# Nine instead of seven pairs of an up projection by Strassen's products, some of them one behind another, and silu as one activation

## The chip, the cores and the metric

The kernel runs on one core of a Trainium2 chip. The metric is the device time of one execution in microseconds (us). Three timed runs of the kernel before took 867.1, 866.76 and 868.9 us; their median is 867.1. One more execution was profiled, and its trace is what the views below are made from.

## The reference

The reference is one block of a decoder: a recurrent branch and an attention branch that are merged, and then a feed-forward part with a short causal convolution. The change touches the feed-forward part alone:

```
h2 = rmsnorm(x, norm2_g[l]) * (1.0 + scale2) + shift2
u = causal_dwconv(h2 @ w_up[l], ffn_conv_w[l], ffn_conv_b[l])
u_gate, u_val = u[..., :D_FF], u[..., D_FF:]
x = x + gate2 * ((jax.nn.silu(u_gate) * u_val) @ w_down[l])
```

There are 512 tokens, a model width of 1024 and D_FF = 2816; the convolution has three taps along the tokens. All of it is float32.

## The kernel before, in words

**Products in three passes.** TensorE multiplies in fp32r. To keep float32's precision, `split` (L207) cuts an operand into two parts: ScalarE copies it into fp32r (L210), and VectorE subtracts this from the operand to get the rest (L211). A product then is three matmuls: high by high, high by low, low by high (`mm3`, L247 to L249).

**The up projection.** The 2 x 2816 output channels lie on partitions, in 44 tiles of 128 channels by 512 tokens. A pair `j` (0 to 21) is the gate's tile and the value's tile of the same 128 channels, `2j` and `2j+1`. A tile that is done the plain way takes eight blocks of the inner dimension by three passes, 24 matmuls of 512 columns, and its weights are two units of 128x512 that `Stream.get` (L226) loads and splits. `project` (L257) issues it. Its two tiles are in two banks of PSUM of the tag "acc", and `conv` (L1155) reads them there: one activation with scale and bias on ScalarE (L1157) and two scalar_tensor_tensor on VectorE (L1159). `gate` (L1161) makes silu(gate) x value and splits the result for the down projection: a tanh on ScalarE (L1162), two scalar_tensor_tensor on VectorE (L1163, L1164), and a split.

**A pair by Strassen's products.** The pairs in the list `STRASSEN` see the pair's two weight tiles and the two halves of the tokens as a 2 x 2 product of blocks, in Winograd's form: seven products of four blocks of the inner dimension by three passes, each 12 matmuls of 256 columns (`prod`, L1102). `weights` (L1111) loads the pair's two weight tiles into two buffers `raw` (L1115, L1116), makes four sums of quarters on VectorE (L1120, L1121, L1122, L1124) and splits seven quarters. The token side's sums (`Ts`) are made once, while pairs 0 to 3 run. `front` (L1128) issues six products into three banks, x of the tag "acc" and y and z of the tag "tr", and combines them in the pair's working tile `w`; `last_product` (L1149) adds the seventh, from the quarter `q22`, on top of what is in bank x. The combined outputs lie in `w` in SBUF, and `conv` and `gate` work from there.

**The order of the work.** Before the feed-forward part, the order of every engine's queue is written out by hand (`QUEUES`, `queue_order`). Within it a planner orders each engine's instructions by priorities; `high_priority(offset=AHEAD)` moves `weights` and the loads and splits of `project` 100 places ahead. TensorE's order is fixed by `in_order` (L253): each product is issued behind the last instruction noted in `chained`. The loop over pairs (L1170) issues `front` of a Strassen pair and goes on; the next pair is a plain one, and after that pair's first tile come the Strassen pair's `last_product`, its two `conv` and its `gate`. The next Strassen pair's `weights` are called at the plain pair's second tile. So Strassen pairs and plain pairs take turns from pair 5 to pair 17.

**Buffers that are waited for.** Split quarters and units lie in two buffers of the tag "whl" and two of "whg", by turns; `raw` has three buffers of 512 KB; the working tiles `w` (tag "Y") have two; "acc" and "tr" have three banks each.

**After it** comes the down projection, 12 of its 22 blocks of the inner dimension plainly and ten by Strassen's products (`f_forms`, `w_forms`, `strassen_down`), then the last norm and the output.

Of the kernel before, what the change touches and what calls it, by code (L numbers as in the profile page):

```python
# [14 lines left out]
AF = mybir.ActivationFunctionType  # L15
ALU = mybir.AluOpType
ADD, SUB, MUL = ALU.add, ALU.subtract, ALU.mult
# [73 lines left out]
AHE = 100  # L91
SQB = (1, 0, 2, 3)
EARLY = 4
STRASSEN = (5,7,9,11,13,15,17)
G2J = 18
ROOM = -1

# [74 lines left out]
def block_kernel(ctx, tc, a):  # L172
    nc = tc.nc
    V, S, G, PE = nc.vector, nc.scalar, nc.gpsimd, nc.tensor
# [25 lines left out]
    def raw():  # L200
        return st(sb, "raw", RAW, [P, 1024])
# [49 lines left out]
    chained = None  # L251

    def in_order(on=True):  # L253

        return tc.issue_after(chained) if on and chained is not None else ExitStack()
# [322 lines left out]
    with phase("p_attn") as p1:  # L578
# [5 lines left out]
        w = st(p1, "v", 2, [P, 2, T])  # L584
# [200 lines left out]
        for hd in range(HEADS):  # L785
            g, i = divmod(hd, 4)
# [65 lines left out]
    with phase("p_rnn") as p2:  # L852
# [87 lines left out]
        for m in range(8):  # L940
            b = bank("tr")
            project(b, wpr, m, NR, lambda k: yr[k], ahead=AHM, order=m >= ORDM)
            t = tr_[m]
# [22 lines left out]
        for k in range(NK):  # L966
            with tc.high_priority(offset=AHO):
                w, _ = wo.get(k * T)
# [3 lines left out]
            chained = last  # L972
# [12 lines left out]
        for t in range(4):  # L985
            b = bank("fil" if t % 2 else "gm")
            for k in range(NK):
                with tc.high_priority(offset=AHO):
                    w, _ = wo.get((NK + k) * T)
                with in_order(ORDO):  # L990
                    last = mm_tok(b, mg[k], tok(t), w, k == 0, k == NK - 1)
            chained = last
# [45 lines left out]
    with phase("p_ffn") as p3:  # L1038
# [4 lines left out]
        for s in (slice(0, T // 2), slice(T // 2, T)):  # L1043
            for m in range(EARLY):
                for k in range(NK):
                    with tc.high_priority(offset=AHE):
                        w, o = wu.get((m * NK + k) * P)
                    with in_order(ORDE):
                        last = mm3(ub[m][:, s], w, o, P, h2[:, k], s, k == 0, k == NK - 1)
                chained = last  # L1050
# [6 lines left out]
        HT, HK = T // 2, NK // 2  # L1057
# [18 lines left out]
        Ts = []  # L1076
# [25 lines left out]
        def prod(out, w, x, start, stop):  # L1102
            for k, (xk, s) in enumerate(x):

                wh, wl = w[:, 0, k * P:k * P + P], w[:, 1, k * P:k * P + P]
                for e, (we, xe) in enumerate(((wh, 0), (wh, 1), (wl, 0))):
                    last = PE.matmul(out, we, xk[:, xe, s], start=start and k == 0 and e == 0,  # L1107
                                     stop=stop and k == HK - 1 and e == 2, skip_group_check=True).ins
            return last

        def weights(j):  # L1111

            with tc.high_priority(offset=AHEAD):
                r0, r1 = raw(), raw()
                dma(r0, a["w_up"][2 * j])  # L1115
                dma(r1, a["w_up"][2 * j + 1])  # L1116
                w11, w12, w21, w22 = r0[:, :T], r0[:, T:], r1[:, :T], r1[:, T:]
                s1 = st(p3, "ff", NF, [P, T])
                q11, q12 = quarter(j, w11), quarter(j, w12)
                V.tensor_tensor(s1, w21, w22, ADD)  # L1120
                V.tensor_tensor(w21, w11, w21, SUB)  # L1121
                V.tensor_tensor(w11, s1, w11, SUB)  # L1122
                qs1, qs2 = quarter(j, s1), quarter(j, w11)
                V.tensor_tensor(w12, w12, w11, SUB)  # L1124
                qs4, qs3, q22 = quarter(j, w12), quarter(j, w21), quarter(j, w22)
            return q11, q12, qs1, qs2, qs4, qs3, q22

        def front(w, q11, q12, qs1, qs2, qs4, qs3, q22):  # L1128

            nonlocal chained  # L1130
            X, Y_, Z = bank("acc"), bank("tr"), bank("tr")
            x, y_, z = (b[:, :HT] for b in (X, Y_, Z))
            p1, p2, p5 = w[:, 2, :HT], w[:, 2, HT:], w[:, 3, :HT]
            with in_order():
                prod(x, q11, h_part(0, 0), True, False)
                prod(y_, q12, h_part(1, 0), True, True)
                S.activation(p1, x, AF.Copy)
                prod(z, qs1, Ts[0], True, False)
                V.tensor_tensor(w[:, 0, :HT], y_, p1, ADD)
                prod(x, qs2, Ts[1], False, False)  # L1140
                S.activation(p5, z, AF.Copy)
                prod(z, qs4, h_part(1, 1), False, True)
                S.activation(p2, x, AF.Copy)
                V.tensor_tensor(w[:, 0, HT:], z, p2, ADD)
                chained = prod(x, qs3, Ts[2], False, False)
                V.tensor_tensor(w[:, 1, HT:], x, p5, ADD)
            return x, q22

        def last_product(w, x, q22):  # L1149
            nonlocal chained  # L1150
            with in_order():
                chained = prod(x, q22, Ts[3], False, True)
            S.activation(w[:, 1, :HT], x, AF.Copy)

        def conv(j, i, u, src):  # L1155
            cj = i * NF + j
            S.activation(u, src, AF.Identity, scale=vc("fw", 2 * 2 * NF + cj), bias=vc("fb", cj))  # L1157
            for d in (1, 2):
                V.scalar_tensor_tensor(u[:, d:], src[:, :T - d], vc("fw", (2 - d) * 2 * NF + cj), u[:, d:], MUL, ADD)  # L1159

        def gate(u0, u1, t):  # L1161
            S.activation(t, u0, AF.Tanh, scale=0.5)  # L1162
            V.scalar_tensor_tensor(u0, t, 1.0, u0, ADD, MUL)  # L1163
            V.scalar_tensor_tensor(u0, u0, 0.5, u1, MUL, MUL)  # L1164
            o = hl(p3, "ff", NF)
            split(o, 0, T, u0)
            ff.append(o)

        left = None
        for j in range(NF):  # L1170
            w = st(sb, "Y", 2, [P, 4, T])
            if j in STRASSEN:
                left = (j, w) + front(w, *ahead)
                continue
            convs = []
            for i in range(2):
                if 2 * j + i < EARLY:
                    b = ub[2 * j + i]
                else:
                    b = bank("acc")  # L1180
                    project(b, wu, 2 * j + i, NK, lambda k: h2[:, k], ahead=AHEAD, order=ORD)
                if left and i == 0:
                    last_product(*left[1:])
                    for e in range(2):
                        conv(left[0], e, left[1][:, 2 + e, :], left[1][:, e, :])
                    gate(left[1][:, 2, :], left[1][:, 3, :], left[1][:, 0, :])
                    left = None
                if i and j + 1 in STRASSEN:
                    ahead = weights(j + 1)
                convs.append((j, i, w[:, i, :], b))  # L1190
            for c in convs:
                conv(*c)
            gate(w[:, 0, :], w[:, 1, :], w[:, 2, :])
            if j < 4:
                Ts.append(next(t_it))
            if j == G2J:
                g2_it = ada2(1, st(sb, "acc4", 1, [P, D]), lambda: st(sb, "R", 4, [P, D]))
            if G2J <= j < G2J + 4:
                next(g2_it)
                g2 = next(g2_it)  # L1200
            if j == G2J + 3:
                ada_row(g2, 1.0)
                fg = st(sb, "R", 4, [P, D])
                dma(fg, a["fg"].partition_broadcast(P))
                V.tensor_scalar(fg[:, T:], fg[:, T:], -0.5, None, MUL)
# [93 lines left out]
        for k in range(KO):  # L1299
            with tc.high_priority(offset=AHEAD):  # L1300
                w, _ = wd.get(k * T)
# [10 lines left out]
        for t in range(4):  # L1312
            w = xf[t]
# [16 lines left out]
        for k in range(KO - LASTK):  # L1330
            with tc.high_priority(offset=AHEAD):
                w, _ = wd.get((NF + k) * T)
# [8 lines left out]
        for part in parts:  # L1341
            t, o, n, b = part
            if o == 0:
                w = st(sb, "Y", 2, [P, 2, T])
# [115 lines left out]
```

## Time and profile before

| what | value |
|---|---|
| median of three timed runs | 867.1 us (866.76 to 868.9) |
| the profiled execution, its own time | 870.13 us |
| its span, first to last instruction | 868.3 us |
| mean granted TensorE clock | 0.994 |
| the 145.5 us from the first Strassen product to the last | 557.5 to 703.0 us of the span |

The profile page gives busy time by engine, the span in 40 slices, DMA queues, the chain of work that ended last, and groups of instructions by line. PE is TensorE's matmuls, PEld its weight loads, DVE VectorE, ACT ScalarE, POOL GpSimd, SP the queue that issues most DMAs. Times in the timeline count from the span's start. A matmul's length in the timeline holds its way through the array and overlaps the next, so a series is measured from the start of one to the start of the next. The same holds, in part, for VectorE: an instruction's length and its distance to the next are two numbers.

### The profile page before, as it was taken

Reading aid. Unit: us, or ns where it says so; the run is one execution under the profiler, and the core shown is the slowest. Engines: PE = TensorE matmul, PEld = TensorE weight load, DVE = VectorE, ACT = ScalarE, POOL = GpSimd, SP = SyncE. Lnnn points to the kernel's source line nnn. Section 1 sums busy time; section 2 is a strip of 40 time slices with the busy share of each in tenths; the row PEclk is TensorE's granted clock in tenths of the full one; section 3 lists DMA queues with packets and bytes.
Section 4 is the critical chain, followed back from the end, with each engine's and each line's share of the span. In section 5 each row is a group of like instructions: output and inputs, shape, how many; then the busy total and the mean of one; then the engine's idle time right before and its main releaser. Section 6 shows DMA issues by size and latency. Waiting matters only on the chain.

```text
span 868.3 us, 12376 instructions
## 1 busy us (share of the span) xinstructions
PE 845.7 (97%) x4432; PEld 698.3 (80%) x4432; DVE 737.1 (85%) x1417; ACT 534.8 (62%) x998; POOL 23.9 (3%) x49
## 2 busy tenths in 40 slices
PE   7999999999999999999999999999999999999995
PEld 4777888878877777777877798888888887889985
DVE  7989888988856899998375679999989999998985
ACT  7485878677745798886244566656666654535533
POOL 0001000001020000000000001000000000000000
PEclk8999999999999999999999999999999999999998
DMA  9913232443463243345324044322322374323332
GB/s 352 352 68 107 72 111 97 125 146 116 145 176 118 82 161 121 122 161 204 94 76 146 25 134 111 98 75 101 105 101 102 102 275 162 97 73 98 100 95 97
DMA packets 34674, 110.72 MB, mean 128 GB/s; under 512 B 4386, under 2 KB 8098, under 8 KB 34612
## 3 DMA queue, kind: packets, MB, share of 16 engines
q1 hardware_dynamic: 32116, 103.60, 35.1%
q0 software_dynamic: 2496, 6.33, 3.4%
q8 instruction: 35, 0.57, 0.3%
q14 instruction: 27, 0.22, 0.1%
HBM read 105.16 MB, written 2.13 MB: 124 GB/s over the span
## 4 chain that ended last, share of the span: by engine, by line
PE 55%; DVE 20%; ACT 10%; DMA 9%; issue 4%; POOL 0%; SPq 0%; ACTq 0%; DVEq 0%; POOLq 0%
PE acc L249 5%; PE acc L248 5%; PE acc L247 5%; PE tr L249 3%; PE tr L247 3%; PE tr L248 3%; DVE whg L211 3%; PE acc L1107 2%; DVE whl L211 2%; DMA wa<-in_w_adat 2%; PE tr L1107 2%; PE tr L749 2%; PE gm L249 2%; DVE Y L1159 1%; PE gm L247 1%
## 5 line engine op out<-in xcount | busy, mean ns | idle before, releaser
L210 ACT ACTIVATE whl<-raw 128x512 fp32r<-128x512 f32 (+2 forms) x149 | 83.6, 566 | 69.6 <-PE tr L249 22.4
L211 DVE TENSOR_TENSOR whl<-raw,whl 128x512 fp32r<-128x512 f32 (+2 forms) x149 | 90.6, 612 | 23.3 <-ACT whl L210 22.8
L210 ACT ACTIVATE whg<-raw 128x512 fp32r<-128x512 f32 x131 | 80.9, 625 | 44.5 <-PE tr L249 9.1
L211 DVE TENSOR_TENSOR whg<-raw,whg 128x512 fp32r<-128x512 f32 x131 | 89.2, 688 | 17.8 <-ACT whg L210 17.4
L726 ACT ACTIVATE P<-P,mx,qsc 128x512 f32<-128x512 f32 (+3 forms) x64 | 41.1, 645 | 17.4 <-DVE mx L722 17.3
L247 PE MATMUL acc<-A,whg 128*128 128x512 f32 x120 | 47.9, 399 | 0.0
L248 PE MATMUL acc<-A,whg 128*128 128x512 f32 x120 | 47.4, 395 | 0.0
L249 PE MATMUL acc<-A,whg 128*128 128x512 f32 x120 | 47.4, 395 | 0.0
L1159 DVE SCALAR_TENSOR_TENSOR Y<-acc,vec,Y 128x511 f32<-128x511 f32 (+1 forms) x58 | 43.0, 745 | 4.1 <-ACT Y L1157 4.1
L248 PE MATMUL acc<-A,whl 128*128 128x512 f32 x104 | 41.1, 395 | 0.0
L247 PE MATMUL acc<-A,whl 128*128 128x512 f32 x104 | 41.1, 395 | 0.0
L249 PE MATMUL acc<-A,whl 128*128 128x512 f32 x104 | 41.1, 395 | 0.0
L249 PE MATMUL gm<-A,whg 128*128 128x512 f32 x88 | 35.2, 400 | 1.9 <-DVE whg L211 1.9
L247 PE MATMUL gm<-A,whg 128*128 128x512 f32 x88 | 35.5, 404 | 0.0
L248 PE MATMUL gm<-A,whg 128*128 128x512 f32 x88 | 35.3, 401 | 0.0
L249 PE MATMUL tr<-A,whl 128*128 128x512 f32 x80 | 32.2, 403 | 1.2 <-DVE whl L211 1.1
L247 PE MATMUL tr<-A,whl 128*128 128x512 f32 x80 | 32.4, 406 | 0.6 <-ACT whl L210 0.6
L719 DVE CUSTOM_DVE_ANT_0 P<-acc,mask 128x384 f32<-128x384 f32 (+3 forms) x64 | 28.5, 486 | 4.0 <-PE acc L716 3.6
L248 PE MATMUL tr<-A,whl 128*128 128x512 f32 x80 | 31.5, 394 | 0.0
L210 ACT ACTIVATE ff<-Y 128x512 fp32r<-128x512 f32 (+1 forms) x27 | 15.9, 590 | 22.0 <-DVE Y L1164 20.8
L211 DVE TENSOR_TENSOR pt<-tr,pt 128x512 fp32r<-128x512 f32 (+1 forms) x48 | 27.5, 596 | 2.1 <-ACT pt L210 1.6
L749 PE MATMUL tr<-pt,v 128*128 128x512 f32 (+3 forms) x128 | 28.2, 328 | 0.1
(603 smaller groups left out, 2524.9 us busy)
## 6 DMA issues: line engine op xcount, KB each, us to landing
raw<-in_w_up SPq DMA_DIRECT2D x44, 512.0 KB, 3.6
raw<-in_w_dn SPq DMA_DIRECT2D x22, 512.0 KB, 3.5
wa<-in_w_adat SPq DMA_DIRECT2D x16, 512.0 KB, 9.4
raw<-in_w_adat SPq DMA_DIRECT2D x16, 512.0 KB, 3.3
raw<-in_w_xr SPq DMA_DIRECT2D x10, 512.0 KB, 3.8
raw<-in_w_pr SPq DMA_DIRECT2D x10, 512.0 KB, 3.6
raw<-in_w_gm SPq DMA_DIRECT2D x8, 512.0 KB, 4.0
raw<-in_w_gr SPq DMA_DIRECT2D x8, 512.0 KB, 3.5
```

Source lines behind the costliest of these rows:

```text
L210: S.activation(h, src, AF.Copy)
L211: return V.tensor_tensor(dst[:, 1, lo_c:lo_c + n], src, h.bitcast(F32), SUB).ins
L247: PE.matmul(out, wh, x[:, 0, xs], start=start, stop=False)
L248: PE.matmul(out, wh, x[:, 1, xs], start=False, stop=False)
L249: return PE.matmul(out, wl, x[:, 0, xs], start=False, stop=stop).ins
L719: V.tensor_tensor_reduce(out=pt[:, POFF[qd]:POFF[qd] + n], in0=sc[qd], in1=mask[:, T - n:], scale=1.0, scalar=-3e38, op0=ADD, op1=ALU.max, ...
L726: S.activation(pq, pq, AF.Exp, scale=qsc[:, qb:qb + 1], bias=mx[:, qb:qb + 1], accum_out=sm[:, qb:qb + 1])
L749: PE.matmul(yb[:, kb * P:], vv, pth[:, part, off:off + n], start=(i == 0 and part == 0), stop=(i == 3 and part == 1))
L1107: last = PE.matmul(out, we, xk[:, xe, s], start=start and k == 0 and e == 0, stop=stop and k == HK - 1 and e == 2, skip_group_check=True).ins
L1159: V.scalar_tensor_tensor(u[:, d:], src[:, :T - d], vc("fw", (2 - d) * 2 * NF + cj), u[:, d:], MUL, ADD)
```

## The change

The list of Strassen pairs goes from 5, 7, 9, 11, 13, 15, 17 to 5, 7, 8, 10, 11, 13, 14, 16, 17. So there are nine, and four times two of them stand one behind the other with a plain pair after them. `front` is cut in two: after its first three products it calls `finish`, which issues what is left of a Strassen pair just before it (its last product, its two convolutions and its gate); where a plain pair comes next, `finish` is called after that pair's first tile, as before. The sum of bank x and p5 (L1146) is taken from a copy `u3` of bank x that ScalarE makes, and no longer from the bank. `weights` of a second pair in a row are called straight after the `front` of the first. And `gate`, for all 22 pairs, takes silu in one activation and multiplies once on VectorE, in place of a tanh and two scalar_tensor_tensor.

```
-STRASSEN = (5,7,9,11,13,15,17)
+STRASSEN = (5,7,8,10,11,13,14,16,17)
...
-            p1, p2, p5 = w[:, 2, :HT], w[:, 2, HT:], w[:, 3, :HT]
+            p1, p2, p5, u3 = w[:, 2, :HT], w[:, 2, HT:], w[:, 3, :HT], w[:, 3, HT:]
             with in_order():
                 prod(x, q11, h_part(0, 0), True, False)
                 prod(y_, q12, h_part(1, 0), True, True)
                 S.activation(p1, x, AF.Copy)
-                prod(z, qs1, Ts[0], True, False)
                 V.tensor_tensor(w[:, 0, :HT], y_, p1, ADD)
+                chained = prod(z, qs1, Ts[0], True, False)
+                S.activation(p5, z, AF.Copy)
+            finish()
+            with in_order():
                 prod(x, qs2, Ts[1], False, False)
-                S.activation(p5, z, AF.Copy)
                 prod(z, qs4, h_part(1, 1), False, True)
                 S.activation(p2, x, AF.Copy)
                 V.tensor_tensor(w[:, 0, HT:], z, p2, ADD)
                 chained = prod(x, qs3, Ts[2], False, False)
-                V.tensor_tensor(w[:, 1, HT:], x, p5, ADD)
+                S.activation(u3, x, AF.Copy)
+            V.tensor_tensor(w[:, 1, HT:], u3, p5, ADD)
             return x, q22
...
         def gate(u0, u1, t):
-            S.activation(t, u0, AF.Tanh, scale=0.5)
-            V.scalar_tensor_tensor(u0, t, 1.0, u0, ADD, MUL)
-            V.scalar_tensor_tensor(u0, u0, 0.5, u1, MUL, MUL)
+            S.activation(t, u0, AF.Silu)
+            V.tensor_tensor(u0, t, u1, MUL)
             o = hl(p3, "ff", NF)
             split(o, 0, T, u0)
             ff.append(o)
...
+        def finish():
+            nonlocal left
+            if left:
+                last_product(*left[1:])
+                for e in range(2):
+                    conv(left[0], e, left[1][:, 2 + e, :], left[1][:, e, :])
+                gate(left[1][:, 2, :], left[1][:, 3, :], left[1][:, 0, :])
+                left = None
...
             if j in STRASSEN:
-                left = (j, w) + front(w, *ahead)
+                now = (j, w) + front(w, *ahead)
+                left = now
+                if j + 1 in STRASSEN:
+                    ahead = weights(j + 1)
                 continue
...
-                if left and i == 0:
-                    last_product(*left[1:])
-                    for e in range(2):
-                        conv(left[0], e, left[1][:, 2 + e, :], left[1][:, e, :])
-                    gate(left[1][:, 2, :], left[1][:, 3, :], left[1][:, 0, :])
-                    left = None
+                if i == 0:
+                    finish()
```

## The prediction

> **What bounds the kernel now.** The first view is the profile's page, for the balance of the engines; the second is the table of busy times by stage, for the stretch that the change touches.
>
> ```profile
> span 868.3 us, 12376 instructions
> PE 845.7 (97%) x4432; PEld 698.3 (80%) x4432; DVE 737.1 (85%) x1417; ACT 534.8 (62%) x998; POOL 23.9 (3%) x49
> ```
>
> ```profile
> 557.50:703.00 145.50, 144.84 (x907) 129.38 (x906) 133.37 (x220) 90.20 (x160) 0.00 (x0) 1.00 0.31 107
> 703.00:742.00 39.00, 39.00 (x169) 31.17 (x168) 38.12 (x60) 19.21 (x31) 0.00 (x0) 1.00 0.55 182
> ```
>
> The columns of the second are the stretch, its length, the busy time of PE, PEld, DVE, ACT and POOL with their instructions, the granted clock, the DMA share and GB/s. From the first Strassen product (557.5) to the last (703.0) TensorE is busy for 144.84 of 145.50 us at full clock, VectorE for 133.37 (92%). So TensorE sets the time, with VectorE close behind. In the 39 us after it VectorE is busy for 38.12 and TensorE still has no gap: 98% of VectorE does not by itself cost time. Busy TensorE time is modelled, so the third view is the timeline of TensorE, read from start to start.
>
> ```profile
> 557.52 1.56 PE L1107 MATMUL acc<-A,whg 128*128 128x256 f32 x12
> 558.92 1.58 PE L1107 MATMUL tr<-A,whl 128*128 128x256 f32 x12
> 566.02 0.40 PE L247 MATMUL acc<-A,whl 128*128 128x512 f32 x1
> 571.62 1.60 PE L1107 MATMUL acc<-R,whg 128*128 128x256 f32 x12
> 573.06 0.40 PE L247 MATMUL acc<-A,whl 128*128 128x512 f32 x1
> 578.66 1.58 PE L1107 MATMUL acc<-A,whl 128*128 128x256 f32 x12
> 685.98 1.56 PE L1107 MATMUL acc<-A,whg 128*128 128x256 f32 x12
> ```
>
> These are pair 5's first product (557.52), the first plain tile of pair 6 (566.02), pair 5's last product (571.62), pair 6's second tile (573.06), and the first products of pairs 7 (578.66) and 17 (685.98). Six products take 566.02 - 557.52 = 8.50 us, the seventh 573.06 - 571.62 = 1.44: a Strassen pair is 9.94 us, a product 1.42. A plain tile takes 571.62 - 566.02 = 5.60, again 578.66 - 573.06 = 5.60: a plain pair is 11.20. A round of one each is 21.14, and the first round took just that. The six rounds from 557.52 to 685.98 took 21.41 on average, 0.27 more each. Where that goes is seen at the next pair:
>
> ```profile
> 582.31 0.68 DVE L1124 TENSOR_TENSOR raw<-raw 128x512 f32<-128x512 f32 x1
> 582.89 0.40 PE L1107 MATMUL acc<-ff,whg 128*128 128x256 f32 x2
> 582.91 1.29 DVE L211 TENSOR_TENSOR whg<-raw,whg 128x512 fp32r<-128x512 f32 x2
> 583.65 1.46 PE L1107 MATMUL acc<-ff,whg 128*128 128x256 f32 x10 [0.37 <-DVE whg L211]
> ```
>
> Two matmuls of the fourth product (qs2) run, the rest wait for VectorE's half of the split: 583.65 - 582.89 is 0.76, less two matmuls of 0.12 gives a stall of 0.52 us. VectorE is late with this quarter, since its queue holds convolutions and gates ahead of it.
>
> **Part 1: two plain pairs become Strassen pairs.** TensorE saves 2 x (11.20 - 9.94) = 2.52 us, on the path, since it is what the stretch waits for. Taking 2.5.
>
> **Part 2: silu in one activation.** VectorE loses one instruction of 128x512 for each pair. Its prices, from the grouped lines and from the chain of waits (start, distance to the next, what):
>
> ```profile
> L1164 DVE SCALAR_TENSOR_TENSOR Y<-Y 128x512 f32<-128x512 f32 x22 | 15.1, 689 | 0.2
> L211 DVE TENSOR_TENSOR whl<-raw,whl 128x512 fp32r<-128x512 f32 x51 | 34.6, 688 | 2.1 <-ACT whl L210 1.8
> L1159 DVE SCALAR_TENSOR_TENSOR Y<-acc,vec,Y 128x511 f32<-128x511 f32 x28 | 20.8, 744 | 0.0
> L1139 DVE TENSOR_TENSOR Y<-tr,Y 128x256 f32<-128x256 f32 x7 | 2.9, 418 | 0.0
> L1162 ACT ACTIVATE Y<-Y 128x512 f32<-128x512 f32 x22 | 13.9, 631 | 14.2 <-DVE Y L1159 14.2
> ```
>
> ```profile
> 577.15 0.67 DVE Y L1159
> 580.53 0.60 DVE whl L211
> ```
>
> and for 256 columns from the timeline (start, length, what), two starts that follow one another:
>
> ```profile
> 653.99 0.42 DVE L1144 TENSOR_TENSOR Y<-tr,Y 128x256 f32<-128x256 f32 x1
> 654.32 0.41 DVE L1146 TENSOR_TENSOR Y<-acc,Y 128x256 f32<-128x256 f32 x1
> ```
>
> An instruction of 0.69 us is followed by the next after 0.60, one of the convolution's 0.744 after 0.67, one of 256 columns after 0.33: in a queue that is full, these distances are the price. The activation stays one of 128x512, 0.63. On VectorE 22 x 0.60 = 13.2 us go. On the path only those stalls of TensorE go that VectorE's lateness makes: 0.27 us in each of seven rounds, 1.9 us. Since two gates (0.60 each, 1.2 us together) lie ahead of each late quarter and the stall shown was 0.52, I take all of the 1.9 as gone where pairs still take turns; next in line is TensorE itself. The bounds are 0 and 1.9.
>
> **Part 3: what the runs of two cost.** VectorE's bill by those distances, with the new gate of two instructions (product and split): a Strassen pair has 7 splits and 4 sums at 0.60 (6.60), 3 combinations at 0.33 (0.99), 4 of the convolution at 0.67 (2.68), and the gate (1.20), 11.47 us, against 9.94 on TensorE. A plain pair has 4 splits (2.40), the convolution (2.68) and the gate, 6.28, against 11.20. A round was 11.47 + 6.28 + 2 x 0.60 = 18.95 of 21.14 us (90%). A run with its plain pair will be 2 x 11.47 + 6.28 = 29.22 of 31.08 (94%). So VectorE has enough time over a round of three, but in a run it falls 2 x 1.53 = 3.06 us behind, and must put off convolutions and gates. This is tight at two places.
>
> The first is the second pair's weights. Of three buffers of raw weights, the second pair's other half gets the one that the first pair's qs4 releases:
>
> ```profile
> 642.96 1.56 PE L1107 MATMUL acc<-A,whg 128*128 128x256 f32 x12
> 649.07 0.33 SPq L231 DMA_DIRECT2D raw<-in_w_up  x1
> 652.71 0.63 ACT L210 ACTIVATE whl<-raw 128x512 fp32r<-128x512 f32 x1 [0.54 <-DMA raw<-in_w_up]
> ```
>
> In pair 13 this release let SP's next load go 6.1 us after the pair's first product, and its data were there at 9.75 us. Then come the sum s1 (0.69), ScalarE's copy (0.63) and VectorE's rest (0.69) for qs1, some 2.1 us with the hand-overs: ready at 11.85, or at 10.65 if the two gates' 1.2 us are gone from ahead of it. The eighth product ends at 8 x 1.42 = 11.36. So the stall is 0 to 0.5 us in each of four runs; I take 0.2, as the middle of the two cases with a lean to the relieved one: 0.8 us. What follows, the previous pair's last product, gives the next quarter 1.42 us more. SP's queue holds the following plain pair's loads behind this one; that pair's first tile starts at 14 products, 19.9 us, so they are late for nobody.
>
> The second is the next run's fourth product, where the stalls are today. VectorE's spare time there was 21.14 - 18.95 = 2.19 us in 21 and will be 1.86 in 31, while conv and gate of two Strassen pairs must be over before the next `front` takes their working tile. There was 0.27 us lost with 2.19 to spare; I take 0.4 for each of the three restarts at 10, 13 and 16: 1.2 us. The bounds are 0, if the planner's order fits, and 1.5, the deficit of one Strassen pair.
>
> The other edits cost nothing. The copy u3 is a fourth ScalarE copy of 256 columns per pair; ScalarE is busy for 90.20 of 145.50 us. It hides in the three products (4.3 us) between qs3 and the last product that writes the bank; without them its 0.37 would stand on the path:
>
> ```profile
> L1153 ACT ACTIVATE Y<-acc 128x256 f32<-128x256 f32 x7 | 2.6, 366 | 0.0
> ```
>
> p5's copy stands one product earlier in the queue's order but has the same input. The down projection is not touched; it could only start with a lighter VectorE.
>
> **The sum.** -2.5 (products) -1.9 (stalls gone) +0.8 +1.2 (new stalls) = -2.4 us. The profiled execution took 870.13 (span 868.3 and 1.8 around it), 3.0 above the median of the timed runs, so this gives 867.7 for such an execution and 867.1 - 2.4 = 864.7 us for the median. With a measurement of this kernel about 0.3%, 2.6 us, can be told from no change, and this lies just inside.
>
> **A rule that speaks against it.** Two splits in the row at 582.91 took 1.29 us together, not 2 x 0.69. The Trainium skill, page VectorE: DVE Perf Modes, section Terms, says that a flush follows every VectorE instruction and that the next cannot issue until the pipe is empty. Going by that rule, lengths and not distances would be the bill; the trace disagrees in the part by which neighbours overlap, 0.09 us each.
>
> **The rivals.** *No new stall.* The planner orders VectorE's queue so that quarters always come first, and TensorE runs without a gap: -2.5 - 1.9 = -4.4, 862.7 us. For it speaks that TensorE kept going where VectorE was at 98% (the stretch from 703). Against it: the late fourth product came back in most rounds though VectorE had 2 us to spare.
>
> *VectorE becomes the bound in the runs (slower).* The place is the two Strassen pairs of a run. If VectorE can put off nothing, or its instructions do not overlap in a mixed queue, TensorE waits for it. By lengths the bill of a run and its plain pair is 2 x (11 x 0.69 + 3 x 0.42 + 4 x 0.744 + 2 x 0.69) + (4 x 0.69 + 4 x 0.744 + 2 x 0.69) = 33.5 us against 31.08, 2.4 lost in each of four, 9.7: 867.1 - 4.4 + 9.7 = 872.4 us. The rule above is this second form. By distances with no putting off it is 3.06 in each, 12.2: 874.9 us. Slower by more than 2.6 us begins where a run loses 7.0 / 4 = 1.75 us. For it: 94%. Against it: the 98% stretch, and the overlap at 582.91.
>
> *Silu brings table loads.* The profile has
>
> ```profile
> L1162 ACT ACT_TABLE_LOAD x1: 1283/1283/1283, 518.1 to 518.1; - x1
> L884 ACT ACT_TABLE_LOAD x9 | 11.5, 1283 | 0.2
> ```
>
> one load for 22 tanh, with copies and affine activations between them, while line 884 loads nine times. If silu's table held no copy, each gate would bring two loads, 2.57 us, in which the splits wait; with 13 gates in the stretch, half of 33.4 us on the path gives 867.1 - 4.4 + 16.7 = 879.4 us. Page ScalarE: Activation LUTs of the Trainium skill, section Table sets, says that cheap functions such as copy and identity are in every set; by it there is one load, and the tanh row agrees.
>
> That the change doesn't do what it says is no case: TensorE's order is chained by hand.
>
> **How the numbers follow.** My forecast, new stalls of 1 to 4 us (863.7 to 866.7), gets 0.60; of this about 0.16 lies below 864.5, where faster begins. No new stall or under 1 us gets 0.28; VectorE as the bound 0.10; table loads 0.02. So faster 0.44, same 0.46, slower 0.10 (0.44 of the forecast is same, and 0.02 of the bound by VectorE in a weak form; the rest of that case and the table loads are slower). The range goes from 862.6, the rival without stalls, to 868.4, new stalls of 5.7 us, where both tight places stand at their upper bounds (2.0 and 4.5, less a little): it leaves out the 0.12 of the last two cases and a little at the ends.
>
> **What would show it.** Right: 63 products of 12 matmuls in the stretch for 49 before, and a stretch some 2.4 us shorter than its 145.5; the fourth product of pairs 7 and 10 without the split's wait; small waits of the ninth product in pairs 8, 11, 14 and 17 for VectorE or a load; VectorE at some 94% in the stretch. Wrong: waits of TensorE over 1.5 us in each run, more than one table load at the gate's line, a bank of the tag "acc" or "tr" that TensorE waits for, or a gain without any stall left.

## The result and the profile after

The median went from 868.24 us (866.76 to 869.64, 12 runs) to 863.15 us (860.01 to 865.61, 12 runs). The ratio is 0.9945 with a 95% interval of 0.9933 to 0.9958: 4.8 us faster (3.6 to 5.8), where 2.4 were forecast. By the bound of 0.3% it is faster.

The page after, to be held against the two page lines of before, and two stretches in the table of busy times by stage (columns as before): from the first Strassen product to the end of the last, and the 39 us behind it.

```profile
span 862.4 us, 12546 instructions
PE 842.8 (98%) x4504; PEld 700.5 (81%) x4504; DVE 734.3 (85%) x1415; ACT 543.6 (63%) x1021; POOL 23.9 (3%) x49
```

```profile
555.74:697.64 141.90, 141.45 (x973) 130.41 (x972) 132.66 (x223) 96.80 (x178) 0.00 (x0) 1.00 0.33 108
697.64:737.00 39.36, 39.36 (x171) 31.56 (x170) 37.57 (x61) 20.48 (x34) 0.00 (x0) 1.00 0.55 189
```

The stretch with the Strassen pairs is bounded by TensorE as before, at the same clock. VectorE is busy for 132.66 of 141.90 us (93%; 94% were forecast), ScalarE for 96.80 in place of 90.20. The stretch shown for before, 145.50 us, ended too late: its last Strassen product is followed by the next matmul at 701.71, not at 703.0. Between the same two points it took 144.2 us, so the stretch is 2.3 us shorter and not 3.6.

The profiled execution took 864.22 us (its span is 862.4), 5.9 less than that of before. To place those 5.9 us, the timeline of TensorE, first of before and then of after: the first matmul of the up projection and the first of the down projection.

```profile
500.43 0.37 PE L247 MATMUL acc<-A,ff 128*128 128x256 f32 x1
...
741.98 0.39 PE L845 MATMUL acc<-whl,ff 128*128 128x512 f32 x1
```

```profile
498.57 0.37 PE L247 MATMUL acc<-A,ff 128*128 128x256 f32 x1
...
737.82 0.39 PE L845 MATMUL acc<-whl,ff 128*128 128x512 f32 x1
```

Three parts follow. Ahead of the first row nothing was changed, and 1.9 us of the difference lies there (500.43 against 498.57). In the profiles of the twelve other kernels below this row stands between 496.6 and 500.2, so over the fourteen it varies by up to 3.8 us. TensorE, VectorE and ScalarE have the same instructions in the same order up to this row in all of them, so this part isn't put down to the change. (The latest three, 499.95 to 500.43, are kernels with the old list; why is not known.) The up projection went from 741.98 - 500.43 = 241.55 to 737.82 - 498.57 = 239.25 us, 2.3 less. From the down projection to the end of the span it went from 868.27 - 741.98 = 126.29 to 862.45 - 737.82 = 124.63, 1.7 less. So in these two profiles the forecast's -2.4 is nearly what the up projection gained, and the rest stands where no change was expected.

**The up projection in the profile after.** The fourth product of pair 7 (the row of 581.11; in before the one at 582.89, with 0.52 us of stall) follows the third without a gap:

```profile
579.69 1.58 PE L1107 MATMUL tr<-ff,whl 128*128 128x256 f32 x12
581.11 1.60 PE L1107 MATMUL acc<-ff,whg 128*128 128x256 f32 x12
```

The same holds for pairs 10, 13 and 16, up to 0.09 us in 13: the stalls at a run's start are gone. The run of pairs 10 and 11 has two others; the timeline of all engines, cut to the chain of the ninth product (qs1 of pair 11):

```profile
613.06 0.33 SPq L1116 DMA_DIRECT2D raw<-in_w_up  x1
...
616.50 1.58 PE L1107 MATMUL acc<-A,whg 128*128 128x256 f32 x12
617.40 0.69 DVE L1120 TENSOR_TENSOR ff<-raw 128x512 f32<-128x512 f32 x1 [0.79 <-DMA raw<-in_w_up]
618.13 0.63 ACT L210 ACTIVATE whg<-ff 128x512 fp32r<-128x512 f32 x1 [1.05 <-DVE ff L1120]
619.22 0.69 DVE L211 TENSOR_TENSOR whg<-ff,whg 128x512 fp32r<-128x512 f32 x1
619.33 0.40 PE L1107 MATMUL tr<-ff,whg 128*128 128x256 f32 x2
...
619.96 1.45 PE L1107 MATMUL tr<-ff,whg 128*128 128x256 f32 x10 [0.23 <-DVE whg L211]
```

This is the chain that the prediction told: the load is let go at 613.06 and lands before 617.40, then sum, copy and rest. VectorE stood idle for 0.79 us for the load. The rest is done at 619.91, two matmuls after the product began, so TensorE loses 619.96 - 619.33 - 2 x 0.118 = 0.39 us. In the runs of 13 and 16 it is 0.16 and 0.13, in the run of 7 nothing: 0.68 in all.

The second is in the thirteenth product (qs3 of the second pair), and wasn't foreseen. ScalarE and that product in the run of 13, from the timeline:

```profile
655.77 0.82 ACT L1160 ACTIVATE Y<-Y,vec 128x512 f32<-128x512 f32 x1
656.50 0.62 ACT L210 ACTIVATE whl<-raw 128x512 fp32r<-128x512 f32 x1
657.02 0.36 ACT L1145 ACTIVATE Y<-acc 128x256 f32<-128x256 f32 x1
657.43 1.48 PEld L1107 LDWEIGHTS acc<-R,whl 128*128 128x128 f32 x12 [0.27 <-ACT Y L1145]
657.43 1.68 PE L1107 MATMUL acc<-R,whl 128*128 128x256 f32 x12
```

qs3 writes the bank x, which ScalarE must first copy out (p2, L1145). This copy stands in ScalarE's queue behind the activation of a convolution and a split, and ends at 657.38. In three runs it costs 0.23 to 0.24 us, 0.7 in all. The view of the products' line names both waits (it counts the engine's idle time, of which not all is lost):

```profile
  DVE whg L211: 1.0, 4
  ACT Y L1145: 0.8, 3
```

Silu's activation has one table load, as tanh had:

```profile
L1165 ACT ACTIVATE Y<-Y x22: 615/632/635, 517.6 to 735.5; 128x512 f32<-128x512 f32 x22
...
L1165 ACT ACT_TABLE_LOAD  x1: 1283/1283/1283, 516.3 to 516.3; - x1
```

**The end.** The last two of the four output tiles, VectorE and SP's queue in the timeline, of before and of after:

```profile
853.31 2.20 SPq L1358 DMA_DIRECT2D out_y<-Y  x2
...
854.34 0.75 DVE L1356 SCALAR_TENSOR_TENSOR Y<-T,rs,R 128x512 f32<-128x512 f32 x1
...
857.98 0.69 DVE L1348 TENSOR_TENSOR Y<-tr,acc 128x512 f32<-128x512 f32 x1 [2.89 <-DMA out_y<-Y]
```

```profile
848.78 8.21 SPq L1369 DMA_DIRECT2D out_y<-Y  x3
849.80 0.75 DVE L1367 SCALAR_TENSOR_TENSOR Y<-T,rs,R 128x512 f32<-128x512 f32 x1
...
851.50 0.69 DVE L1359 TENSOR_TENSOR Y<-tr,acc 128x512 f32<-128x512 f32 x1 [0.94 <-DMA out_y<-Y]
853.38 0.42 DVE L1359 TENSOR_TENSOR Y<-fil,acc 128x256 f32<-128x256 f32 x1 [0.47 <-DMA out_y<-Y]
```

The output tiles have two buffers of the tag "Y". In before, VectorE's first work on the next output tile waits 2.89 us for a buffer whose store must end; after, two such waits of 0.94 and 0.47 us stand in its place. That is 2.89 - 1.41 = 1.5 of the 1.7 us. No line of this part was edited; how the list of pairs comes to change which buffer a tile gets was not traced.

### The profile page after: what moved, and what is told of

It reads as the page before. It is cut to its first block, busy times and chain, and to the rows that moved or that the text cites. A ratio compares the mean times of both kernels' runs of the same rounds, so it can differ in the third digit from the quotient of the medians.

```text
span 862.4 us, 12546 instructions
## 1 busy us (share of the span) xinstructions
PE 842.8 (98%) x4504; PEld 700.5 (81%) x4504; DVE 734.3 (85%) x1415; ACT 543.6 (63%) x1021; POOL 23.9 (3%) x49
## 4 chain that ended last, share of the span: by engine, by line
PE 59%; DVE 22%; ACT 9%; DMA 5%; issue 4%; POOL 0%; SPq 0%; DVEq 0%; ACTq 0%; POOLq 0%
PE acc L249 4%; PE acc L248 4%; PE acc L247 4%; DVE whg L211 3%; PE tr L249 3%; PE tr L247 3%; PE tr L248 3%; DVE whl L211 2%; DVE Y L1162 2%; PE tr L749 2%; PE gm L249 2%; PE acc L845 2%; PE acc L847 2%; PE acc L846 2%; PE gm L248 2%
## 5 line engine op out<-in xcount | busy, mean ns | idle before, releaser
L1162 DVE SCALAR_TENSOR_TENSOR Y<-acc,vec,Y 128x511 f32<-128x511 f32 (+1 forms) x50 | 37.1, 744 | 9.0 <-ACT Y L1160 8.8
L247 PE MATMUL acc<-A,whg 128*128 128x512 f32 x104 | 41.5, 399 | 0.0
L249 PE MATMUL acc<-A,whg 128*128 128x512 f32 x104 | 41.1, 395 | 0.0
L248 PE MATMUL acc<-A,whg 128*128 128x512 f32 x104 | 41.1, 395 | 0.0
L248 PE MATMUL acc<-A,whl 128*128 128x512 f32 x88 | 34.8, 395 | 0.0
L247 PE MATMUL acc<-A,whl 128*128 128x512 f32 x88 | 34.7, 395 | 0.0
L249 PE MATMUL acc<-A,whl 128*128 128x512 f32 x88 | 34.7, 395 | 0.0
L1162 DVE SCALAR_TENSOR_TENSOR Y<-Y,vec 128x511 f32<-128x511 f32 (+1 forms) x36 | 26.6, 746 | 0.2
```

Source lines behind the costliest of these rows:

```text
L247: PE.matmul(out, wh, x[:, 0, xs], start=start, stop=False)
L248: PE.matmul(out, wh, x[:, 1, xs], start=False, stop=False)
L249: return PE.matmul(out, wl, x[:, 0, xs], start=False, stop=stop).ins
```

## The experiments

No kernel leaves part of the computation out. Ratios are to the kernel before, with their 95% interval; a difference to the changed kernel is the difference of two ratios times 868 us, and is uncertain by 1.4 to 1.9 us. "Up" is the up projection and "end" what follows it in the span, both read as above. "Lost" is the sum, over the up projection, of what the distance between two matmuls' starts has over 0.118 us (256 columns) or 0.2325 (512), where it is more than 0.06; the last two columns are against the changed kernel.

| kernel | up | lost | end | ratio | up and end | by ratio |
|---|---|---|---|---|---|---|
| before | 241.55 | 2.54 | 126.29 | 1 | +4.0 | +4.8 |
| changed | 239.25 | 2.60 | 124.63 | 0.9945 (0.9933 to 0.9958) | 0 | 0 |
| e1_silu_only | 240.32 | 1.10 | 125.90 | 0.9975 (0.9959 to 0.9991) | +2.3 | +2.6 |
| e2_runs_tanh | 242.96 | 6.40 | 124.81 | 0.9988 (0.9974 to 1.0002) | +3.9 | +3.7 |
| e3_old_list | 240.29 | 1.10 | 125.90 | 0.9980 (0.9965 to 0.9995) | +2.3 | +3.0 |
| e6_none | 248.29 | 0.43 | 124.58 | 1.0056 (1.0041 to 1.0071) | +9.0 | +9.6 |
| e7_triples | 241.69 | 6.23 | 124.58 | 0.9973 (0.9963 to 0.9983) | +2.4 | +2.4 |
| e4_ten | 245.01 | 9.78 | 124.78 | 1.0007 (0.9993 to 1.0022) | +5.9 | +5.4 |
| e11_no_u3 | 240.82 | 4.33 | 124.57 | 0.9974 (0.9960 to 0.9988) | +1.5 | +2.5 |
| e5_own_raw | 238.77 | 2.04 | 124.57 | 0.9939 (0.9924 to 0.9954) | -0.5 | -0.5 |
| e7_before_tail | 242.25 | 3.24 | 124.79 | 0.9993 (0.9980 to 1.0007) | +3.2 | +4.2 |
| e10_after_tail | 238.78 | 1.95 | 124.37 | 0.9950 (0.9932 to 0.9968) | -0.7 | +0.4 |
| e12_raw_tail | 238.90 | 2.04 | 124.35 | 0.9950 (0.9932 to 0.9969) | -0.6 | +0.4 |
| e13_bad_tail | 239.07 | 2.33 | 125.40 | 0.9958 (0.9943 to 0.9973) | +0.6 | +1.1 |

The last two columns agree within 1.1 us in every row, so the traces can be used to say where the time is. The up projection itself differs by 0.5 to 0.7 us between two kernels in which it is the same code (changed and e10_after_tail, before and e7_before_tail); smaller differences in a single profile are not read.

**Silu alone.** The new gate in the kernel before:

```
-            S.activation(t, u0, AF.Tanh, scale=0.5)
-            V.scalar_tensor_tensor(u0, t, 1.0, u0, ADD, MUL)
-            V.scalar_tensor_tensor(u0, u0, 0.5, u1, MUL, MUL)
+            S.activation(t, u0, AF.Silu)
+            V.tensor_tensor(u0, t, u1, MUL)
```

> The kernel before with the new gate alone: seven Strassen pairs in turns with plain ones, silu in one activation and one product. My theory: TensorE's lost time in the rounds (3.1 us between the first Strassen product and the last one's start) comes from VectorE's queue and goes for the most part, 1 to 2 us faster than before. Rival: VectorE's instructions were off the path, within 0.5 us of before, and the whole gain of the change comes from the two pairs.

Measured: 2.2 us faster than before (0.8 to 3.6). In the profile the lost time falls from 2.54 to 1.10 and the up projection by 1.2. The stalls did go, and this term is real, at 1.2 to 2.2 us where 1.9 was taken. (The expectation's 3.1 us fit the stretch of 145.50 us less 7 x 9.94 + 6.5 x 11.20 = 142.38; with the stretch of 144.2 they are 1.8.)

**The runs with the old gate.** The changed kernel with the three removed lines above back in their place:

> The changed kernel with the old gate of a tanh and two scalar_tensor_tensor. My theory: with 0.60 us more per pair VectorE's bill for a run and its plain pair is 31.0 of 31.1 us, TensorE waits for it in each run, and of the 2.5 us that the two pairs save at least 2 are lost again: 0 to 3 us slower than before. Rival: the two parts simply add, and without silu the gain is that of the two pairs alone, 2.5 us faster than before.

Measured: 1.0 us faster than before (from 2.3 faster to 0.2 slower), between the two expectations. In the profile the up projection is 1.4 us longer than that of before, with 6.40 us of lost time against 2.54: there the 2.5 us that two pairs save are lost again and more, and the end, 1.5 us shorter, is what remains. VectorE is at 140.14 of 145.80 us (96%), and the fourth product of every run waits for it again. The stretch, and the fourth and ninth product in the run of 10:

```profile
554.43:700.23 145.80, 142.92 (x974) 130.64 (x972) 140.14 (x236) 95.25 (x179) 0.00 (x0) 1.00 0.32 105
```

```profile
612.18 0.40 PE L1107 MATMUL acc<-ff,whg 128*128 128x256 f32 x2
613.01 1.46 PE L1107 MATMUL acc<-ff,whg 128*128 128x256 f32 x10 [0.43 <-DVE whg L211]
...
619.99 0.40 PE L1107 MATMUL tr<-ff,whg 128*128 128x256 f32 x2
621.01 1.46 PE L1107 MATMUL tr<-ff,whg 128*128 128x256 f32 x10 [0.62 <-DVE whg L211]
```

613.01 - 612.18 less two matmuls of 0.118 is 0.59 us, 621.01 - 619.99 less the same 0.78. Silu alone gave 2.2 and the runs alone 1.0; both together gave 4.8. By the times alone the 1.6 us between 3.2 and 4.8 are not clear of their uncertainty. The up projections say it more plainly: 1.2 shorter with silu, 1.4 longer with the runs, 2.3 shorter with both. The two parts are not independent: the lighter gate pays for the runs.

**The cut and the copy without the runs.** The changed kernel with `STRASSEN = (5,7,9,11,13,15,17)`:

> The changed kernel with the old list 5, 7, 9, 11, 13, 15, 17: new gate, the cut in front and the copy u3, but no two pairs in a row. My theory: the cut and the copy cost nothing, so the time is that of silu alone within 0.5 us. Rival: the copy on ScalarE or the new place of the instructions moves the time by more than 0.5 us against silu alone.

Measured: 1.7 us faster than before, silu alone 2.2; up and lost are the same to 0.03 us. The cut of `front` and the copy u3 cost nothing where pairs take turns, as forecast.

**No Strassen pair.** The changed kernel with `STRASSEN = ()`:

> The changed kernel with an empty list: 22 plain pairs, no Strassen product, the token side's sums still made. By the price read from TensorE, 1.26 us per pair and no stalls (VectorE's bill for a plain pair is 6.3 of 11.2 us): 9 x 1.26 less the 1.4 us of listed stalls, some 10 us slower than the changed kernel, and 6 to 7 us slower than silu alone with seven. Rival: if Strassen pairs cost more than their products (bank and buffer waits of under 0.1 us that do not show), 7 us or less.

Measured: 9.6 us slower than the changed kernel, 7.0 slower than silu alone. In the profile the up projection is 9.04 longer and loses 2.60 - 0.43 = 2.17 us less to waits. So nine pairs save 9.04 + 2.17 = 11.2 on TensorE, 1.25 each. The prediction had 11.20 - 9.94 = 1.26.

**Longer runs.** Ten pairs, in two runs of two and two of three (the expectation counts three of three), `STRASSEN = (5,6,8,9,10,12,13,14,16,17)`:

> The changed kernel with ten pairs of which three runs have three (5, 6, 8, 9, 10, 12, 13, 14, 16, 17). TensorE would be 1.26 us shorter. VectorE's bill for a run of three with its plain pair is 3 x 11.47 + 6.28 = 40.7 of 41.0 us on TensorE (99%). My theory: VectorE falls 4.6 us behind in such a run, which is more than it can put off, the ninth and the fourth products wait in each run, and the kernel is 1 to 5 us slower than the changed one. Rival: pair 4's failure came from its early place alone, and ten pairs placed later are 1 us faster.

Measured: 2.4 us slower than the changed kernel with one pair more, which by the price above is worth 1.25. The lost time goes from 2.60 to 6.23. The timeline of VectorE and TensorE in the run of 8, 9 and 10:

```profile
608.95 0.68 DVE L1120 TENSOR_TENSOR ff<-raw 128x512 f32<-128x512 f32 x1
609.57 0.69 DVE L211 TENSOR_TENSOR ff<-Y,ff 128x512 fp32r<-128x512 f32 x1
610.35 0.50 PE L1107 MATMUL tr<-ff,whg 128*128 128x256 f32 x2 [0.70 <-ACT whg L210]
...
611.52 1.46 PE L1107 MATMUL tr<-ff,whg 128*128 128x256 f32 x10 [0.67 <-DVE whg L211]
```

These are qs1 of the third pair. The chain is that of the ninth product (raw load, sum at 608.95, copy, rest), but it is late for the whole product and not only for its third matmul: TensorE loses 0.85 us ahead of 610.35 and 0.83 ahead of 611.52, where the ninth product, of the second pair, lost 0.52; in the run of 12 the third pair loses 0.87 and 0.82. This is the deficit that the prediction feared for runs of two; it comes with runs of three.

**An earlier tenth pair.** Pair 4 added in front, `STRASSEN = (4,5,7,8,10,11,13,14,16,17)`:

> The changed kernel with pair 4 added to the list (4, 5, 7, 8, 10, 11, 13, 14, 16, 17), ten pairs. If TensorE sets the time everywhere, another 1.26 us faster than the changed kernel. Rival: at pair 4 VectorE is still busy with the token side's sums (19.1 to 19.8 of 20 us busy between 520 and 560 us in the kernel before), the run 4, 5 stalls by its deficit of 3 us, and the time is 0 to 2 us slower than the changed kernel.

Measured: 5.4 us slower than the changed kernel, more than either expectation. While pairs 0 to 3 run, VectorE and ScalarE also make the token side's sums; with pair 4 as a Strassen pair these come due at once. The table by stage for 540 to 560 us, and TensorE's products there:

```profile
540.00:560.00 20.00, 17.11 (x124) 15.79 (x123) 19.81 (x32) 12.17 (x23) 0.00 (x0) 0.97 0.16 54
```

```profile
554.60 0.51 PE L1107 MATMUL tr<-ff,whl 128*128 128x256 f32 x2 [0.59 <-ACT whl L210]
555.69 1.45 PE L1107 MATMUL tr<-ff,whl 128*128 128x256 f32 x10 [0.57 <-DVE whl L211]
558.12 0.38 PE L1107 MATMUL acc<-R,whg 128*128 128x256 f32 x1 [0.99 <-ACT R L210]
559.23 2.08 PE L1107 MATMUL acc<-R,whg 128*128 128x256 f32 x8 [0.72 <-DVE R L211]
```

VectorE is busy for 19.81 of 20 us and TensorE for 17.11: it waits for the weights' quarters (whl) and for the token side's last sum (R). The rival of the early place holds, and was too low. Not all of it is waiting: right behind these waits the granted clock is 0.62 from 558 to 562 us, and from 559.61 to 562.37 the matmuls start every 0.213 us in place of 0.118, some 1.2 us more.

**Without the copy u3.** The third sum read from bank x itself, as before:

```
-                S.activation(u3, x, AF.Copy)
-            V.tensor_tensor(w[:, 1, HT:], u3, p5, ADD)
+                V.tensor_tensor(w[:, 1, HT:], x, p5, ADD)
```

> The changed kernel without the copy u3: VectorE reads bank x itself, as before. My theory: the copy is what keeps the last product of a first pair, three products later, from waiting for VectorE's queue; without it TensorE waits there in each run, 0.5 to 2 us slower in all. Rival: VectorE reads the bank in time and ScalarE has one copy less in front of p2's, so it is the same or up to 0.7 us faster.

Measured: 2.5 us slower than the changed kernel, at or above the upper end of what was expected. VectorE and TensorE's last products in the run of 10:

```profile
620.68 0.69 DVE L211 TENSOR_TENSOR whl<-raw,whl 128x512 fp32r<-128x512 f32 x1
621.28 0.42 DVE L1148 TENSOR_TENSOR Y<-acc,Y 128x256 f32<-128x256 f32 x1
621.76 1.63 PE L1107 MATMUL acc<-R,whl 128*128 128x256 f32 x12 [0.95 <-DVE Y L1148]
...
626.54 1.68 PE L1107 MATMUL acc<-R,whl 128*128 128x256 f32 x12 [0.38 <-ACT Y L1145]
```

The last product writes bank x and may not begin before VectorE has read it. In a run VectorE gets to that read at 621.28, behind a split, and TensorE loses 1.11 us; 1.18 in the run of 16. With the copy, ScalarE frees the bank and VectorE may be late. So the copy is worth some 2 us in runs, and nothing without them (e3_old_list).

**The second pair's own buffer for raw weights.** The changed kernel, with the other half of a second pair in a buffer that no earlier pair holds:

```
-                r0, r1 = raw(), raw()
+                r0, r1 = raw(), st(sb, "acc4", 1, [P, D]) if j - 1 in STRASSEN else raw()
```

> The changed kernel with a buffer of its own (acc4, idle in this stage) for the second half of a second pair's raw weights, so that its load needs no release by the first pair. My theory: the waits of the ninth product (0.39, 0.16 and 0.13 us in three of the four runs) come from that load; they go, and the stretch gets 0.7 us shorter. Rival: VectorE's queue is late anyway and the ninth product waits as before, no change; or the stall moves to the next products.

Measured: 0.5 us faster than the changed kernel, which its interval doesn't part from nothing. The waits of the thirteenth product are down to at most 0.10 us, and those of the ninth stand elsewhere: 0.24 us at 587.07 and 0.77 at 681.4, where it now waits for VectorE's read of a bank of the tag "tr". Freeing the load moves the wait more than it removes it. Undecided by the time.

**The end.** Four kernels ask whether the wait for an output buffer is worth time. In three the output tiles come from the three large `raw` buffers, so that none waits for a store: before, changed, and changed with the edit of e5_own_raw.

```
-                w = st(sb, "Y", 2, [P, 2, T])
+                w = raw().rearrange("p (e n) -> p e n", e=2)
```

> The kernel before with the four output tiles taken from the three raw buffers in place of the two of tag Y; nothing else differs. My theory: in the kernel before the third output tile takes the buffer that the second output's DMA still reads and VectorE waits 2.9 us for it, and in the changed kernel it happens to take the first output's (waits of 0.9 and 0.5 us), so 1.3 to 1.7 us of the change's gain come from the planner's choice of a buffer at the very end. Then this kernel is 1.3 us or more faster than before. Rival: the end is set by the fourth tile's chain behind TensorE's last product, and the time stays within 0.3 us.

> The changed kernel with the same output tiles from the raw buffers. If the end holds part of the change's gain by accident, this one gains less than the kernel before does by the same edit: 0.3 to 1.0 us against the changed kernel, and its distance to the kernel before with that edit is what the change is worth in the up projection alone, 2.3 us by the traces. Rival: it gains as much as the kernel before does, and the end has no part in the change's gain.

> The changed kernel with both edits, the own raw buffer and the output tiles from the raw buffers. If both theories hold, 1.0 to 1.7 us faster than the changed kernel, some 6 us faster than before.

In the fourth the changed kernel is given a wait that it doesn't have: the third output tile is written into the second's buffer.

```
-            if o == 0:
-                w = st(sb, "Y", 2, [P, 2, T])
+            if o == 0 and t != 2:
+                w = raw().rearrange("p (e n) -> p e n", e=2)
```

> The changed kernel with its end made like that of the kernel before: the third output tile is written into the second one's buffer and so waits for the second output's DMA (the first and the fourth have raw buffers). If that wait is a part of the time, as the traces of the kernel before have it, this is 1.3 to 1.7 us slower than the changed kernel. Rival: the timed comparison of the kernel before with raw buffers for its outputs showed 0.6 us (and no change within its interval), so the wait is hidden outside the profile, and the time stays within 0.5 us of the changed kernel.

Measured: before gains 0.6 us by it (from 1.7 to -0.6), where 1.3 or more were expected, though the wait of 2.9 us is gone from its profile and the end is 1.5 shorter. The changed kernel gains nothing (0.4 slower, within the interval), with the end 0.3 shorter. Both edits together are no better than the changed kernel, where 1.0 to 1.7 were expected. The kernel with the added wait is 1.1 slower, with the end 0.8 longer. The first and the last point the forecast way, the other two don't, and none is clear of zero. The last does not repeat the end of before either: the third tile's sum is as late as there (115.9 us behind the down projection's first matmul, 116.0 in before), but the fourth tile's first half goes ahead of it (115.1, 117.3 in before).

The expectation of the changed kernel with raw output tiles names one more comparison: between it and the kernel before with the same edit, where neither waits for a store and the ends take 124.37 and 124.79 us. There the change is still worth 3.7 us by the ratios, uncertain by some 2, and the up projections of these two profiles differ by 242.25 - 238.78 = 3.5. So by this most of the 4.8 us is there without the wait at the end, and the 2.3 that the expectation had for it lies low, though not outside the uncertainty.

Another reading of the table helps in part. In VectorE's waits the line for an output buffer has one of two forms, here of e3_old_list and of the changed kernel:

```profile
DVE Y L1359 <- DMA out_y<-Y: 2.7, 1, 2.7
```

```profile
DVE Y L1359 <- DMA out_y<-Y: 1.4, 2, 0.9
```

One wait of 2.7 to 2.9 us is found in the three kernels with the old list (before, e1_silu_only, e3_old_list), whose end takes 125.9 to 126.3; two short ones in all with another list and these output tiles, ends of 124.6 to 124.8. So it is no accident of one execution but goes with the list of pairs. Those three kernels take 2.5, 1.5 and 2.0 us more than the changed one beyond what the up projection explains (4.8 - 2.3, 2.6 - 1.1, 3.0 - 1.0), the six others with tiles of the tag "Y" -0.4 to 0.9. That speaks for a worth of 1.5 to 2 us, though each of these numbers holds a single profile's up projection, which differs by 0.5 to 0.7 us for the same code. The direct trial (0.6 us) and the comparison without the wait (4.8 - 3.7 = 1.1) speak for less. It stays open how much of the shorter end the timed runs contain.

## Why the prediction came out as it did

| term of the sum | forecast | in the profile |
|---|---|---|
| two pairs by Strassen's products | -2.5 | -2.5 (1.25 each, e6_none) |
| stalls gone through silu | -1.9 | -1.2 to -2.0 (e1_silu_only, e3_old_list, against before and e7_before_tail) |
| ninth product of a run | +0.8 | +0.5 to +0.7 (changed, e10_after_tail, e13_bad_tail) |
| fourth product at the restarts | +1.2 | 0 to +0.1 |
| thirteenth product, ScalarE's copy | not told | +0.6 to +0.7 (the same three) |
| the up projection | -2.4 | -2.3 (-2.3 to -3.5 with all profiles of the same code) |
| the end | 0 | -1.7 |

In the two profiles first compared the working of the up projection came out right in its sum, and in the products and the ninth product also term by term. For silu's term the prediction put 0.27 us in each round down to VectorE's lateness in one known place. With silu alone 1.10 us of lost time stays, in gaps of at most 0.13 us each; whether 1.9 was too much is not settled, since two profiles of the up projection of before differ by 0.7 us.

The restarts' term was wrong. It rested on the bill of 29.22 us in 31.08, which was right (93% measured), and on the step that with less time to spare the old stall must come back. This step goes against the prediction's own Part 2, which took that stall as gone because two gates ahead of the late quarter each lose 0.60 us; they do so at a restart too. VectorE's queue at the fourth product of the run of 10, of after (product at 612.20):

```profile
610.54 0.68 DVE L1124 TENSOR_TENSOR raw<-raw 128x512 f32<-128x512 f32 x1
611.14 1.29 DVE L211 TENSOR_TENSOR whg<-raw,whg 128x512 fp32r<-128x512 f32 x2
...
613.74 0.74 DVE L1162 SCALAR_TENSOR_TENSOR Y<-acc,vec,Y 128x510 f32<-128x510 f32 x1
```

and with the old gate, of e2_runs_tanh (product at 612.18):

```profile
612.27 1.29 DVE L211 TENSOR_TENSOR whg<-raw,whg 128x512 fp32r<-128x512 f32 x2
...
614.68 0.74 DVE L1162 SCALAR_TENSOR_TENSOR Y<-acc,vec,Y 128x510 f32<-128x510 f32 x1
```

The order is the same in both, and in before too, where this split starts at 582.91 and the convolution's part at 585.32: the planner lets the quarter pass each time. What differs is when the split starts: 612.20 - 611.14 = 1.06 us ahead of the product in after, 612.27 - 612.18 = 0.09 behind it with the old gate. These 1.15 us are about the two times 0.60 that Part 2 had counted.

In place of the restarts' stall stood a wait on an engine that the prediction had counted as free, ScalarE: at 68% in the stretch, a copy of 0.36 us stood behind two other instructions. These two errors offset each other in part, so that the sum came so near is partly luck.

A second step failed, for the total: "The down projection is not touched". Its code is not, but its output tiles share the buffers "Y" with the pairs, and in the profiles the wait for them is 1.3 to 1.5 us shorter with every other list than the old one. In the two profiles first compared -2.3 and -1.7 are 4.0 of the 4.8 measured; the remaining 0.8 is less than the interval's half width. How the 4.8 divides is not settled: without the wait at the end the change is worth 3.7, uncertain by some 2, so the up projection may have gained more than was forecast and the end less than the profiles have. The time of 863.15 us lies next to the rival without new stalls (862.7), but not for its reason: new stalls of 1.4 us are in the profile. Nor does its distance from the forecast 864.7 tell how near the gain came: over twelve runs before took 868.24 us, not the 867.1 of three.

The slower rival, VectorE as the bound in the runs, had its place right and its price too high. By instruction lengths each run would have lost 2.4 us; the runs lose 0 to 0.6 each (0.39 + 0.23 in the run of 10). Of the page VectorE: DVE Perf Modes of the Trainium skill, section Terms, it was said that by its flush lengths would be the bill: the trace of after disagrees as that of before did (the row at 610.54 is 0.68 us long, and the next starts 0.60 behind it). Where VectorE's load goes up a little more, with the old gate (96%) or in runs of three, the rival begins to show, with 6.40 and 6.23 us of lost time in place of 2.60.

Table loads: one. That is as was said of the cheap functions by the page ScalarE: Activation LUTs of the Trainium skill, section Table sets, and the trace agrees (x1 at the gate's line). The copy u3 cost nothing, as told; that the runs need it, for some 2 us, was not seen.

The direction given as likeliest, no change (0.46 against 0.44 for faster), did not come: the forecast gain of 2.4 lay just inside the bound of 2.6, the measured 4.8 lies outside.

## What to carry to other kernels

A bill of an engine over a round tells whether its work fits, and not which instruction comes late: look at which instruction the bounding engine waits for, in each queue, ScalarE's short copies included, and at what the change takes away or adds ahead of that one. Two edits that each move little can need each other, so test them alone and together before one is dropped. And when a list or an order changes, look through the whole span for buffers that are shared with later code, since a wait can come or go where no line was edited.

## What was not expected of the hardware

- The start of the up projection, behind the same code, stands between 496.6 and 500.4 us in fourteen profiles. Two profiles' spans can't be compared to under 4 us without being cut into parts. Part of it is the clock: from 10 to 22 us the granted clock is 0.72 in seven of them (before and after among these), 0.86 in three and 1.00 in four, for the same instructions.
- ScalarE's 631 ns for tanh over 128x512 is 632 for silu, with one table load of 1283 ns for 22 of them, though copies and affine activations stand between.
- Where TensorE was held up most, in e4_ten, with four gaps of 0.74 to 1.16 us within 5 us, the granted clock was 0.62 from 558 to 562 us and 1.00 again from 566 on. From the first Strassen product to the last it is 1.00 in before, after, e2_runs_tanh and e11_no_u3, though the last has single gaps of up to 1.18 us.
